# First loads by k tile, two heads side by side in the SSD product, and a boundary and a last tile moved: a two-layer hybrid trunk on one core

## The chip, the core and the metric

The kernel runs on one core of a Trainium2 chip. The metric is the device time of one execution in microseconds (us), as the median of several runs. Engines are called PE (TensorE; PEld is its weight load), DVE (VectorE), ACT (ScalarE), POOL (GpSimd) and SP (SyncE, which here only issues DMAs).

## What is computed

Two layers of a hybrid decoder, batch 1, 256 tokens, width 1024, all in float32. With 256 tokens there is one attention block and one SSD chunk, so the block selection and the state carried between chunks fall away:

```python
h = rms_norm(x, ln_w); proj = h @ w_in          # q, k, v, gate, z, x/B/C, dt
q, k = rms_norm(q, q_norm_w), rms_norm(k, k_norm_w)
attn = softmax(causal(q @ k.T - slope * distance)) @ v * silu(g_attn)   # 8 heads of 128
xs, bm, cm = split(silu(causal_conv4(xbc)))
dt = softplus(dt_raw + dt_bias); a_cs = cumsum(-exp(a_log) * dt)
decay = exp(where(causal, a_cs[l] - a_cs[s], -inf))
y = (cm @ bm.T * decay) @ (xs * dt) + d_skip * xs                       # 16 heads of 64
y = rms_norm(y * silu(z), groups=2)
x = x + concat(attn, y) @ w_out
```

## The kernel before, in words

Every large product is made of three fp32r matmuls, because each operand is split into a rounded part and the rest: high by high, low by high, high by low. Class `Weights` loads the weights in pieces of two k tiles (`raw`, 348 or 512 columns) into four buffers by DMAs on SP's queue (L78), casts a piece on ACT to `wh` (L92) and subtracts on DVE to `wl` (L94); pieces 0 and 4 are subtracted on POOL (`ON_POOL`). A `raw` buffer comes free when its subtraction is done, and then the next load is issued. Up to eight pieces are kept ready.

At the start SP issues the transposed x (`xT`, four DMAs of two k tiles) and `raw` 0 to 3 in turns, then x itself (`x_sb`); ACT issues one DMA for all parameters (`par_sb`, L136). Ten warm-up matmuls run meanwhile (L152). `first_tokens` (L277) makes `hr` (ACT, scaled by `ln_w`) and `lr` (DVE: `xT` is multiplied in place, then `hr` is subtracted), two k tiles at a time. The v columns are computed from these at once, in three groups v0, v1, v2, without the rms scale; `first_scale` (L287) takes the scale `rs0` from x on ACT, DVE and POOL, and the v results leave PSUM with it (L572). `first_norm` (L297) spreads the scale by a matmul with ones (`rg`, L307) and makes `hT` and `lT`, which all other products of the layer read.

In the SSD part four heads make a quarter (`ssd_quarter`): for each head a product of 256 columns (`e_lo`, L481) and one of 128 columns (`e_hi`, L483), both with 64 weight columns, go to one half of the partitions of `yp`. Each is fp32 and runs as two passes in the trace.

At the end of a layer W_out is read in three stages `oa`, `ob`, `oc`; token half t = 0 is finished first. `pre_norm` (L241) then norms the new x: `hn` on DVE and ACT, `yield wait`, eight transposes on PE (`tp`, L263), `hw` on DVE, `hT` on ACT, `lT` on DVE. A wait counts calls of `tick`, one for each piece of weights. Outside the regions of `manual_schedule` the framework's scheduler sets the order on each engine, and `urgent()` raises a priority in it. Each DMA signals one of eight semaphores (`DMAHW0` to `DMAHW7`), and the ninth waits until the first that used the same one has landed.

Of the kernel before, what the change touches and what calls it, by code (L numbers as in the profile page):

```python
# [15 lines left out]
P = 128  # L16
S = 256
# [31 lines left out]
class Weights:  # L49
# [22 lines left out]
    def load(self, upto):  # L72
        while self.nload <= min(upto, len(self.loads) - 1):
            off, wd = self.loads[self.nload]
            n = KR * wd
            t = self.raw_pool.tile([P, KR, 512], F32, tag="raw", name=f"raw{self.nload}")
            src = self.w[off:off + P * n].rearrange("(p k n) -> p k n", p=P, k=KR)
            self.nc.sync.dma_start(t[:, :, :wd], src)  # L78
            self.raw[self.nload] = t
            self.nload += 1  # L80

    def pump(self, upto=None):
        nc = self.nc
        upto = len(self.subs) if upto is None else upto
        while self.prepped < upto and self.prepped - self.freed < NB:
            i = self.prepped
            li, s, wd = self.subs[i]
            self.load(li + (RAWB - 1 if s == 0 else RAWB - 1))
            src = self.raw[li][:, s * KS:(s + 1) * KS, :wd]
# [18 lines left out]
WARM = 10  # L108
ON_POOL = (0, 4)
URGENT = 400  # L110
# [3 lines left out]
def hybrid_kernel(ctx: ExitStack, tc: tile.TileContext, x, par, w, out):  # L114
# [24 lines left out]
    for s in range(KT // KS):  # L139
# [58 lines left out]

    def mm_tokens(L, name, ts, lh, ll, pss, start, stop, last):

        i0 = ws.index[(L, name)]
        k0, kt, wd = next((k, n, c) for nm, k, n, c in CHUNKS if nm == name)
        for s in range(kt // KS):
            ws.pump()
            wh, wl = ws.parts[i0 + s]
            for t, ps in zip(ts, pss):
                tl = slice(t * P, (t + 1) * P)
                for kk in range(KS):
                    kl = k0 % KT + s * KS + kk
                    first = start and s == 0 and kk == 0  # L210
                    final = stop and s * KS + kk == kt - 1
                    pe.matmul(ps[:, :wd], lh[:, kl, tl], wh[:, kk, :wd], start=first, stop=False)  # L212
                    pe.matmul(ps[:, :wd], ll[:, kl, tl], wh[:, kk, :wd], start=False, stop=False)  # L213
                    pe.matmul(ps[:, :wd], lh[:, kl, tl], wl[:, kk, :wd], start=False, stop=final)  # L214
            if last:
# [61 lines left out]
    def first_tokens(s, hr, lr):  # L277

        ks = slice(s * KS, (s + 1) * KS)
# [17 lines left out]
    def first_norm(rs, hT, lT):  # L297
# [149 lines left out]
    def ssd_quarter(L, pr, x2, dth, ac, nac, cb, cm, dsh):  # L447
# [27 lines left out]
        for i in range(2):  # L475
            for r in range(2):
                j = 2 * i + r
                h = 4 * pr + j
                xs = slice(j * 64, (j + 1) * 64)
                o = slice(r * 64, (r + 1) * 64)  # L480
# [51 lines left out]
    for L in range(NL):  # L532
        pc = L * NPAR
        if L == 0:
# [3 lines left out]
            lv = keep.tile([P, KT, S], F32R, tag="kT", name="lr")  # L538
            with tc.manual_schedule(engines={mybir.EngineType.Activation, mybir.EngineType.DVE}):
                for s in range(KT // KS):  # L540
                    first_tokens(s, hv, lv)
                    ws.pump(s + 1)
            rs0 = small.tile([P, 2], F32, tag="rs0", name="rs0", bufs=1)
# [101 lines left out]

        po = {}
        for j in range(2):
            for t in range(2):
                po[t, j] = ps_p.tile([P, 512], F32, tag="ps_p", name=f"o{t}{j}")
                mm_tokens(L, f"oa{j}", (t,), ah, al, (po[t, j],), True, False, t == 1)  # L650
        drain()
        for j in range(2):
            for t in range(2):
                mm_tokens(L, f"ob{j}", (t,), sh, sl, (po[t, j],), False, False, t == 1)
        region = tc.manual_schedule(engines={mybir.EngineType.PE})
        for t in range(2):
# [3 lines left out]
            for j in range(2):  # L660
                mm_tokens(L, f"oc{j}", (t,), sh, sl, (po[t, j],), False, True, t == 1)
                for a, b in [(0, 256), (256, 512)] if L == NL - 1 and t == j == 1 else [(0, 512)]:
                    cs = slice(j * 512 + a, j * 512 + b)
                    xs = x_sb[t][:, cs]
                    with urgent():
                        dve.tensor_tensor(xs, xs, po[t, j][:, a:b], ALU.add)
                    if L == NL - 1:
# [66 lines left out]
```

## Time and profile before

| what | us |
|---|---|
| three runs, median | 463.7 |
| lowest and highest run | 462.63, 464.36 |
| the profiled execution's own time | 463.97 |
| its span, first to last instruction | 461.9 |
| PE busy in the span | 451.5 |
| DVE busy | 348.0 |
| ACT busy | 280.3 |
| POOL busy | 31.6 |

The profile is of one execution. Times in it count from the first instruction; some 2 us lie around the span. Matmuls are pipelined: one of 512 columns is shown longer than the distance to the next, so costs are read from starts. In a timeline row the brackets give the engine's idle time before the row and what ended it.

### The profile page before, as it was taken

Reading aid. Unit: us, or ns where it says so; the run is one execution under the profiler, and the core shown is the slowest. Engines: PE = TensorE matmul, PEld = TensorE weight load, DVE = VectorE, ACT = ScalarE, POOL = GpSimd, SP = SyncE. Lnnn points to the kernel's source line nnn. Section 1 sums busy time; section 2 is a strip of 40 time slices with the busy share of each in tenths; the row PEclk is TensorE's granted clock in tenths of the full one; section 3 lists DMA queues with packets and bytes.
Section 4 is the critical chain, followed back from the end, with each engine's and each line's share of the span. In section 5 each row is a group of like instructions: output and inputs, shape, how many; then the busy total and the mean of one; then the engine's idle time right before and its main releaser. Section 6 shows DMA issues by size and latency. Waiting matters only on the chain.

```text
span 461.9 us, 7752 instructions
## 1 busy us (share of the span) xinstructions
PE 451.5 (98%) x2900; PEld 403.7 (87%) x2900; DVE 348.0 (75%) x625; ACT 280.3 (61%) x567; POOL 31.6 (7%) x31
## 2 busy tenths in 40 slices
PE   5999999999999999999999999999999999999996
PEld 5998878899998999888799977889999888998885
DVE  4877854889999878957366685776999898789611
ACT  5757758896668546535355765977767674555400
POOL 2200210200000000110000021020000000011000
PEclk8899999999999999999999999999999999999999
DMA  8688884632453355555164988561525263455201
GB/s 268 201 260 286 282 315 181 228 95 95 168 158 115 103 184 181 183 182 142 48 181 128 311 266 305 203 206 62 162 85 188 92 184 115 143 199 176 99 23 70
DMA packets 26213, 79.43 MB, mean 172 GB/s; under 512 B 2592, under 2 KB 9152, under 8 KB 25664
## 3 DMA queue, kind: packets, MB, share of 16 engines
q1 hardware_dynamic: 26032, 78.82, 52.2%
q8 instruction: 23, 0.38, 0.3%
q14 instruction: 14, 0.11, 0.1%
q10 hardware_dynamic: 144, 0.12, 0.1%
HBM read 77.85 MB, written 1.08 MB: 171 GB/s over the span
## 4 chain that ended last, share of the span: by engine, by line
PE 91%; DMA 3%; DVE 3%; ACT 1%; POOL 1%; issue 0%; SPq 0%; DVEq 0%; POOLq 0%
PE o L212 6%; PE o L214 6%; PE o L213 6%; PE xb L231 4%; PE xb L232 4%; PE xb L230 4%; PE z L231 3%; PE z L232 3%; PE k L212 3%; PE g L230 3%; PE g L232 3%; PE q L213 3%; PE k L213 3%; PE g L231 3%; PE z L230 3%; PE k L214 3%
## 5 line engine op out<-in xcount | busy, mean ns | idle before, releaser
L92 ACT CAST wh<-raw 128x1024 fp32r<-128x1024 f32 (+2 forms) x144 | 144.3, 1004 | 68.6 <-PE o L213 21.5
L94 DVE TENSOR_TENSOR wl<-raw,wh 128x1024 fp32r<-128x1024 f32 (+2 forms) x142 | 164.2, 1167 | 28.3 <-ACT wh L92 27.1
L230 PE MATMUL xb<-hT,wh 128*128 128x256 f32 x192 | 56.0, 292 | 0.0
L231 PE MATMUL xb<-lT,wh 128*128 128x256 f32 x192 | 54.9, 286 | 0.0
L232 PE MATMUL xb<-hT,wl 128*128 128x256 f32 x192 | 54.6, 285 | 0.0
L230 PEld LDWEIGHTS xb<-hT,wh 128*128 128x128 f32 x192 | 36.3, 189 | 0.3
L231 PEld LDWEIGHTS xb<-lT,wh 128*128 128x128 f32 x192 | 36.2, 189 | 0.2
L232 PEld LDWEIGHTS xb<-hT,wl 128*128 128x128 f32 x192 | 36.2, 189 | 0.1
L231 PE MATMUL g<-lT,wh 128*128 128x256 f32 x128 | 36.0, 281 | 0.0
L230 PE MATMUL g<-hT,wh 128*128 128x256 f32 x128 | 35.9, 280 | 0.0
L232 PE MATMUL g<-hT,wl 128*128 128x256 f32 x128 | 35.8, 280 | 0.0
L231 PE MATMUL z<-lT,wh 128*128 128x256 f32 x128 | 35.7, 279 | 0.0
L232 PE MATMUL z<-hT,wl 128*128 128x256 f32 x128 | 35.6, 278 | 0.0
L230 PE MATMUL z<-hT,wh 128*128 128x256 f32 x128 | 35.5, 277 | 0.0
L431 DVE SCALAR_TENSOR_TENSOR cv<-rw,par_sb,cv 128x256 f32<-128x256 f32 x72 | 31.5, 479 | 4.8 <-ACT cv L428 4.8
L172 POOL TENSOR_TENSOR rr<-se,mhalf 128x4 f32<-128x4 f32 x16 | 18.0, 1123 | 126.5 <-DVE se L328 90.7
L212 PE MATMUL k<-wh,hT 128*128 128x512 f32 x64 | 25.5, 398 | 0.0
L212 PE MATMUL o<-wh,ah 128*128 128x512 f32 x64 | 25.5, 398 | 0.0
L213 PE MATMUL k<-wh,lT 128*128 128x512 f32 x64 | 25.4, 397 | 0.0
L214 PE MATMUL k<-wl,hT 128*128 128x512 f32 x64 | 25.3, 395 | 0.0
L213 PE MATMUL o<-wh,al 128*128 128x512 f32 x64 | 25.2, 394 | 0.0
L212 PE MATMUL o<-wh,sh 128*128 128x512 f32 x64 | 25.2, 394 | 0.0
(182 smaller groups left out, 1123.3 us busy)
## 6 DMA issues: line engine op xcount, KB each, us to landing
raw<-in_w_dram SPq DMA_DIRECT2D x120, 512.0 KB, 4.4
raw<-in_w_dram SPq DMA_DIRECT2D x16, 348.0 KB, 3.7
cb<-cd SPq DMA_DIRECT2D x4, 1024.0 KB, 8.3
raw<-in_w_dram SPq DMA_DIRECT2D x8, 344.0 KB, 4.0
xT<-in_w_dram SPq DMA_DIRECT2D x4, 256.0 KB, 5.6
x<-in_x_dram SPq DMA_DIRECT2D x2, 512.0 KB, 7.5
out_dram<-x SPq DMA_DIRECT2D x3, 256.0 KB, 2.0
out_dram<-x SPq DMA_DIRECT2D x2, 128.0 KB, 1.8
```

What stands on the lines that cost most here:

```text
L92: nc.scalar.copy(h[:, :, :wd], src)
L94: sub.tensor_tensor(lo[:, :, :wd], src, h[:, :, :wd].bitcast(F32), ALU.subtract)
L172: pool.tensor_tensor(o, i, mhalf[:, :n], ALU.pow)
L212: pe.matmul(ps[:, :wd], lh[:, kl, tl], wh[:, kk, :wd], start=first, stop=False)
L213: pe.matmul(ps[:, :wd], ll[:, kl, tl], wh[:, kk, :wd], start=False, stop=False)
L214: pe.matmul(ps[:, :wd], lh[:, kl, tl], wl[:, kk, :wd], start=False, stop=final)
L230: pe.matmul(o, wh[:, kk, cs], lh[:, k, :], start=(k == 0 and c == 0), stop=False)
L231: pe.matmul(o, wh[:, kk, cs], ll[:, k, :], start=False, stop=False)
L232: pe.matmul(o, wl[:, kk, cs], lh[:, k, :], start=False, stop=(k == KT - 1 and c == 1))
L431: dve.scalar_tensor_tensor(cv[:, c, :], rw[:, c, k:k + S], cw(k), cv[:, c, :], ALU.mult, ALU.add)
```

## The change

- **First loads.** `raw` 0 comes by k tile (two DMAs on SP); `xT` moves to ACT's queue, in five DMAs, with a small DMA of `ln_w` of layer 0 between. x and the rest of the parameters are issued on SP behind `raw` 6.
- **First work.** Piece 0 is cast and subtracted by k tile; all subtractions are on DVE. `lr` is made in one DVE operation for a k tile, so `xT` stays unscaled and `first_norm` multiplies by `ln_w` and the scale in eight operations of one k tile instead of two of four.
- **Table.** A one-column Tanh on ACT (`table`) stands ahead of the first real activation.
- **SSD product.** The two heads of a pair take turns: both long products, then both short ones.
- **Boundary.** The waits of `pre_norm` go from 2 to 3 (t = 0) and from 7 to 5 (t = 1).
- **Last columns.** The last output tile of the last layer is computed as two of 256 columns in two PSUM banks, one after the other in each stage.

```diff
+            for ks in self.steps(self.nload):
+                self.nc.sync.dma_start(t[:, ks, :wd], src[:, ks, :])
+    def steps(i):
+        return [slice(k, k + 1) for k in range(KR)] if i == 0 else [slice(0, KR)]
...
-            nc.scalar.copy(h[:, :, :wd], src)
-            sub = nc.gpsimd if i in ON_POOL else nc.vector
-            sub.tensor_tensor(lo[:, :, :wd], src, h[:, :, :wd].bitcast(F32), ALU.subtract)
+            for ks in self.steps(i):
+                nc.scalar.copy(h[:, ks, :wd], src[:, ks, :wd])
+                nc.vector.tensor_tensor(lo[:, ks, :wd], src[:, ks, :wd],
+                                        h[:, ks, :wd].bitcast(F32), ALU.subtract)
...
-    nc.scalar.dma_start(par_sb, par)
+    nc.scalar.dma_start(xT[:, 0:1, :], xsrc[:, 0:1, :])
+    nc.scalar.dma_start(par_sb[:, C_LN:C_LN + KT], par[:, C_LN:C_LN + KT])
+    nc.scalar.dma_start(xT[:, 1:2, :], xsrc[:, 1:2, :])
+    for s in range(1, KT // KS):
         ks = slice(s * KS, (s + 1) * KS)
-        nc.sync.dma_start(xT[:, ks, :], xsrc[:, ks, :])
-        ws.load(s)
-    for t in range(2):
-        nc.sync.dma_start(x_sb[t], x[t * P:(t + 1) * P, :])
+        nc.scalar.dma_start(xT[:, ks, :], xsrc[:, ks, :])
+    ws.load(RAWB - 1)
...
+    table = const.tile([P, 1], F32, name="table")
+    act.activation(table, ones[:, 0:1], AF.Tanh)
...
         for k in range(s * KS, (s + 1) * KS):
-            act.activation(hr[:, k, :], xT[:, k, :], AF.Copy, scale=par_sb[:, C_LN + k:C_LN + k + 1])
-        dve.tensor_tensor(xT[:, ks, :], xT[:, ks, :],
-                          par_sb[:, C_LN + s * KS:C_LN + (s + 1) * KS].unsqueeze(2)
-                          .to_broadcast([P, KS, S]), ALU.mult)
-        dve.tensor_tensor(lr[:, ks, :], xT[:, ks, :], hr[:, ks, :].bitcast(F32), ALU.subtract)
+            ln = par_sb[:, C_LN + k:C_LN + k + 1]
+            act.activation(hr[:, k, :], xT[:, k, :], AF.Copy, scale=ln)
+            dve.scalar_tensor_tensor(lr[:, k, :], xT[:, k, :], ln, hr[:, k, :].bitcast(F32),
+                                     ALU.mult, ALU.subtract)
...
-            dve.tensor_tensor(xT[:, ks, :], xT[:, ks, :],
-                              rg[:, 0:S].unsqueeze(1).to_broadcast([P, 4, S]), ALU.mult)
+            for k in range(half * 4, half * 4 + 4):
+                dve.scalar_tensor_tensor(xT[:, k, :], xT[:, k, :], par_sb[:, C_LN + k:C_LN + k + 1],
+                                         rg[:, 0:S], ALU.mult, ALU.mult)
...
         for i in range(2):
-            for r in range(2):
-                j = 2 * i + r
-                pe.matmul(yp[o, i * S:(i + 1) * S], xd[:, 0, xs], e_lo[:, j, :],
-                          start=True, stop=False)
-                pe.matmul(yp[o, i * S + 128:(i + 1) * S], xd[:, 1, xs], e_hi[:, j, :],
-                          start=False, stop=True)
+            for hi in range(2):
+                for r in range(2):
+                    j = 2 * i + r
+                    c0 = i * S + hi * P
+                    pe.matmul(yp[o, c0:(i + 1) * S], xd[:, hi, xs],
+                              e_hi[:, j, :] if hi else e_lo[:, j, :],
+                              start=(hi == 0), stop=(hi == 1))
...
-            resume(pre_norm(L, 1, hT, lT, msum[1], 7))
+            resume(pre_norm(L, 1, hT, lT, msum[1], 5))
...
+                po[t, j] = [((0, 512), ps_p.tile([P, 512], F32, tag="ps_p", name=f"o{t}{j}"))]
+                if L == NL - 1 and t == j == 1:
+                    po[t, j] = [((0, 256), po[t, j][0][1]), ((256, 512), bank("o11b"))]
...
-                resume(pre_norm(L + 1, 0, hT, lT, msum[0], 2))
+                resume(pre_norm(L + 1, 0, hT, lT, msum[0], 3))
```

**Order on ACT at the start**, with the semaphores that an instruction waits for (`DMAHW` of a DMA's landing). Before:

```order
L136 DMA par_sb<-in_par_dram 128x236
L281 ACT_TABLE_LOAD [waits DMAHW1_49]
L281 ACTIVATE hr<-xT,par_sb 128x256 [waits DMAHW0_49]
L394 ACTIVATE ea<-par_sb 128x16
L92 CAST wh_139<-raw_90 128x2x348 [waits DMAHW2_49]
```

With the change:

```order
L144 DMA xT<-in_w_dram 128x256
L145 DMA par_sb<-in_par_dram 128x8
L146 DMA xT<-in_w_dram 128x256
L149 DMA xT<-in_w_dram 128x512
L149 DMA xT<-in_w_dram 128x512 [waits DMAHW1_49]
L149 DMA xT<-in_w_dram 128x512 [waits DMAHW2_49]
L156 ACT_TABLE_LOAD
L156 ACTIVATE table<-ones 128x1 [waits DVE_49]
L290 ACTIVATE hr<-xT,par_sb 128x256 [waits DMAHW3_49,DMAHW0_49]
L290 ACTIVATE hr<-xT,par_sb 128x256 [waits DMAHW5_49]
L99 CAST wh_141<-raw_94 128x348 x2
```

The table load stood behind one DMA issue and the wait for the first `xT`; now it stands behind six issues, the last two of which wait for `DMAHW1` and `DMAHW2`. Those are the two halves of `raw` 0, as DVE's subtractions of them show:

```order
L100 TENSOR_TENSOR wl_142<-raw_94,wh_141 128x348 [waits DMAHW1_49,Activation_49]
L100 TENSOR_TENSOR wl_142<-raw_94,wh_141 128x348 [waits DMAHW2_49,Activation_49]
```

**Order on PE in a quarter of the SSD product** (`cb` is `e_lo`, `ehi` is `e_hi`; layer 0, third quarter). Before:

```order
L230 MATMUL g_1943<-hT_129,wh_1604 128x256
L481 MATMUL yp<-cb_0_193,xd 64x256
L466 MATMUL xtp<-ident,x_0_946 128x128
L483 MATMUL yp<-ehi_0_1572,xd 64x128
L481 MATMUL yp<-cb_0_193,xd 64x256
```

With the change:

```order
L240 MATMUL g_1957<-lT_132,wh_1660 128x256
L490 MATMUL yp<-cb_0_201,xd 64x256 x2
L490 MATMUL yp<-ehi_0_1586,xd 64x128 x2
L490 MATMUL yp<-cb_0_201,xd 64x256 x2
L490 MATMUL yp<-ehi_0_1586,xd 64x128 x2
L474 MATMUL xtp<-ident,x_0_960 128x128 x4
```

Before, in all eight quarters, a transpose or a full-width matmul stands behind the first long product. With the change five quarters stand in one piece as here; the other three (layer 0 first, layer 1 first and second) still have two transposes behind the first long product.

**Order on PE at the boundary**, from the transposes of t = 1 to the first v matmuls of t = 1. Before:

```order
L212 MATMUL v_2716<-wh_2655,hT_2568 128x348
L263 MATMUL tp<-ident,hn 128x128 x8
L213 MATMUL v_2716<-wh_2655,lT_2569 128x348
L214 MATMUL v_2716<-wl_2656,hT_2568 128x348
L212 MATMUL v_2716<-wh_2687,hT_2568 128x348
L213 MATMUL v_2716<-wh_2687,lT_2569 128x348
...
L212 MATMUL v_2760<-wh_2501,hT_2568 128x348
L212 MATMUL v_2804<-wh_2631,hT_2568 128x348
L213 MATMUL v_2760<-wh_2501,lT_2569 128x348
```

With the change:

```order
L221 MATMUL v_2730<-wh_2701,hT_2582 128x348
L272 MATMUL tp<-ident,hn 128x128 x8
L222 MATMUL v_2730<-wh_2701,lT_2583 128x348
L223 MATMUL v_2730<-wl_2702,hT_2582 128x348
L221 MATMUL v_2774<-wh_2515,hT_2582 128x348
L221 MATMUL v_2818<-wh_2645,hT_2582 128x348
L222 MATMUL v_2774<-wh_2515,lT_2583 128x348
```

Eight matmuls of t = 0 stood between the transposes and the first matmul that reads their result; now two do. On ACT both copies of v's t = 0 results now stand ahead of the `hT` casts, where one did before. The transposes of t = 0 move from behind the second piece of `oc0` to behind its third.

## Rows read from the trace of the kernel before

**Rows 1.** The page, part 1: busy time of each engine.

```profile
PE 451.5 (98%) x2900; PEld 403.7 (87%) x2900; DVE 348.0 (75%) x625; ACT 280.3 (61%) x567; POOL 31.6 (7%) x31
```

**Rows 2.** Waits of PE: us in total, times, longest.

```profile
PE v L212 <- ACT wh L92: 3.5, 2, 3.2
...
PE tp L263 <- DVE hn L253: 0.8, 1, 0.8
...
PE v L214 <- DVE wl L94: 0.2, 1, 0.2
```

**Rows 3.** Windows: busy (count) of PE, PEld, DVE, ACT, POOL; granted clock; DMA.

```profile
12.00:14.00 2.00, 2.00 (x9) 2.00 (x8) 1.97 (x4) 1.49 (x4) 0.00 (x0) 0.50 1.00 354
14.00:16.00 2.00, 2.00 (x14) 2.00 (x14) 1.97 (x4) 1.98 (x7) 0.00 (x0) 0.96 0.68 193
```

**Rows 4.** Timeline of ACT at the start: start, us.

```profile
5.12 1.28 ACT L281 ACT_TABLE_LOAD   x1 [5.12 <-DMA xT<-in_w_dram]
...
7.33 0.76 ACT L92 CAST wh<-raw 128x696 fp32r<-128x696 f32 x1
```

**Rows 5.** Timeline of PE at the start.

```profile
8.14 0.95 PE L212 MATMUL v<-wh,hr 128*128 128x348 f32 x2 [3.23 <-ACT wh L92]
...
10.35 0.66 PE L214 MATMUL v<-wl,hr 128*128 128x348 f32 x1 [0.58 <-POOL wl L94]
```

**Rows 6.** Chain that ended last, to 27 us: start, us, what.

```profile
0.73 4.51 DMA par_sb<-in_par_dram
...
5.26 0.55 SPq L78
...
5.85 7.16 DMA x<-in_x_dram
...
17.79 0.56 POOL rs L172
```

**Rows 7.** DMA issues, the one at 1.18 us: KB, us to landing.

```profile
raw<-in_w_dram SPq DMA_DIRECT2D x1, 348.0 KB, 5.4
```

**Rows 8.** Timeline of PE, first quarter of the SSD product, layer 0.

```profile
136.88 0.65 PE L481 MATMUL yp<-cb,xd 128*64 128x256 f32 x2
137.45 0.44 PE L364 MATMUL pp<-ident,sc 128*128 128x128 f32 x2
137.82 0.32 PE L483 MATMUL yp<-ehi,xd 128*64 128x128 f32 x1
137.83 0.43 PE L481 MATMUL yp<-cb,xd 128*64 128x256 f32 x1
137.98 0.27 PE L483 MATMUL yp<-ehi,xd 128*64 128x128 f32 x1
...
139.27 0.39 PE L232 MATMUL g<-hT,wl 128*128 128x256 f32 x1
```

**Rows 9.** Timeline of PE at the boundary of the layers.

```profile
242.62 1.03 PE L263 MATMUL tp<-ident,hn 128*128 128x128 f32 x8
243.41 0.41 PE L213 MATMUL v<-wh,lT 128*128 128x348 f32 x1
...
244.77 0.48 PE L212 MATMUL v<-wh,hT 128*128 128x348 f32 x2
245.38 0.42 PE L213 MATMUL v<-wh,lT 128*128 128x348 f32 x1
```

**Rows 10.** Timeline of ACT at the boundary.

```profile
243.98 1.22 ACT L272 CAST hT<-hw 128x512 fp32r<-128x512 f32 x2 [3.11 <-DVE hw L266]
245.10 0.44 ACT L574 COPY v<-v 128x348 f32<-128x348 f32 x1
```

**Rows 11.** Timeline of SP, the last two output DMAs.

```profile
458.58 0.81 SPq L668 DMA_DIRECT2D out_dram<-x  x2
```

**Rows 12.** Chain that ended last, whole span: shares of 461.9 us by line.

```profile
by line: PE o L212 6.2%; PE o L214 6.2%; PE o L213 6.1%; PE xb L231 4.5%; PE xb L232 4.4%; PE xb L230 4.4%; PE z L231 3.3%; PE z L232 3.2%; PE k L212 3.2%; PE g L230 3.2%; PE g L232 3.2%; PE q L213 3.2%; PE k L213 3.2%; PE g L231 3.2%; PE z
```

**Rows 13.** The page, part 5: a DVE group of fused operations on 256 columns.

```profile
L431 DVE SCALAR_TENSOR_TENSOR cv<-rw,par_sb,cv 128x256 f32<-128x256 f32 x72 | 31.5, 479 | 4.8 <-ACT cv L428 4.8
```

More of the change, by code (lines that the diff above doesn't have):

```diff
@@ L77, in load @@
             src = self.w[off:off + P * n].rearrange("(p k n) -> p k n", p=P, k=KR)
-            self.nc.sync.dma_start(t[:, :, :wd], src)
+            for ks in self.steps(self.nload):
+                self.nc.sync.dma_start(t[:, ks, :wd], src[:, ks, :])
             self.raw[self.nload] = t
             self.nload += 1
+    @staticmethod
+    def steps(i):
+        return [slice(k, k + 1) for k in range(KR)] if i == 0 else [slice(0, KR)]
     def pump(self, upto=None):
@@ L87, in pump @@
             li, s, wd = self.subs[i]
-            self.load(li + (RAWB - 1 if s == 0 else RAWB - 1))
-            src = self.raw[li][:, s * KS:(s + 1) * KS, :wd]
+            self.load(li + RAWB - 1)
+            src = self.raw[li]
             h = self.wh_pool.tile([P, KS, 512], F32R, tag="wh", name=f"wh{i}")
             lo = self.wl_pool.tile([P, KS, 512], F32R, tag="wl", name=f"wl{i}")
-            nc.scalar.copy(h[:, :, :wd], src)
-            sub = nc.gpsimd if i in ON_POOL else nc.vector
-            sub.tensor_tensor(lo[:, :, :wd], src, h[:, :, :wd].bitcast(F32), ALU.subtract)
+            for ks in self.steps(i):
+                nc.scalar.copy(h[:, ks, :wd], src[:, ks, :wd])
+                nc.vector.tensor_tensor(lo[:, ks, :wd], src[:, ks, :wd],
+                                        h[:, ks, :wd].bitcast(F32), ALU.subtract)
             self.parts[i] = (h, lo)
@@ L108 @@
 WARM = 10
-ON_POOL = (0, 4)
 URGENT = 400
@@ L197, in drain, with mm_tokens @@
             tick()
-    def mm_tokens(L, name, ts, lh, ll, pss, start, stop, last):
+    def mm_tokens(L, name, ts, lh, ll, pss, start, stop, last, cols=None):
         i0 = ws.index[(L, name)]
         k0, kt, wd = next((k, n, c) for nm, k, n, c in CHUNKS if nm == name)
+        cs = slice(*cols) if cols else slice(0, wd)
         for s in range(kt // KS):
@@ L211, in mm_tokens @@
                     final = stop and s * KS + kk == kt - 1
-                    pe.matmul(ps[:, :wd], lh[:, kl, tl], wh[:, kk, :wd], start=first, stop=False)
-                    pe.matmul(ps[:, :wd], ll[:, kl, tl], wh[:, kk, :wd], start=False, stop=False)
-                    pe.matmul(ps[:, :wd], lh[:, kl, tl], wl[:, kk, :wd], start=False, stop=final)
+                    pe.matmul(ps[:, cs], lh[:, kl, tl], wh[:, kk, cs], start=first, stop=False)
+                    pe.matmul(ps[:, cs], ll[:, kl, tl], wh[:, kk, cs], start=False, stop=False)
+                    pe.matmul(ps[:, cs], lh[:, kl, tl], wl[:, kk, cs], start=False, stop=final)
             if last:
@@ L475, in ssd_quarter @@
         for i in range(2):
[L476 to L484 removed]
+            for hi in range(2):
+                for r in range(2):
+                    j = 2 * i + r
+                    xs = slice(j * 64, (j + 1) * 64)
+                    o = slice(r * 64, (r + 1) * 64)
+                    c0 = i * S + hi * P
+                    pe.matmul(yp[o, c0:(i + 1) * S], xd[:, hi, xs],
+                              e_hi[:, j, :] if hi else e_lo[:, j, :],
+                              start=(hi == 0), stop=(hi == 1))
         for i in range(2):
@@ L538, in hybrid_kernel @@
             lv = keep.tile([P, KT, S], F32R, tag="kT", name="lr")
-            with tc.manual_schedule(engines={mybir.EngineType.Activation, mybir.EngineType.DVE}):
+            with tc.manual_schedule(engines={mybir.EngineType.Activation, mybir.EngineType.DVE,
+                                             mybir.EngineType.SP}):
                 for s in range(KT // KS):
@@ L542, in hybrid_kernel @@
                     ws.pump(s + 1)
+                for t in range(2):
+                    nc.sync.dma_start(x_sb[t], x[t * P:(t + 1) * P, :])
+                nc.sync.dma_start(par_sb[:, 0:C_LN], par[:, 0:C_LN])
+                nc.sync.dma_start(par_sb[:, C_LN + KT:], par[:, C_LN + KT:])
             rs0 = small.tile([P, 2], F32, tag="rs0", name="rs0", bufs=1)
@@ L646, in hybrid_kernel, with mm_out @@
         po = {}
+        def mm_out(name, t, j, lh, ll, start, stop):
+            for i, (c, ps) in enumerate(po[t, j]):
+                mm_tokens(L, name, (t,), lh, ll, (ps,), start, stop,
+                          t == 1 and i == len(po[t, j]) - 1, c)
         for j in range(2):
             for t in range(2):
-                po[t, j] = ps_p.tile([P, 512], F32, tag="ps_p", name=f"o{t}{j}")
-                mm_tokens(L, f"oa{j}", (t,), ah, al, (po[t, j],), True, False, t == 1)
+                po[t, j] = [((0, 512), ps_p.tile([P, 512], F32, tag="ps_p", name=f"o{t}{j}"))]
+                if L == NL - 1 and t == j == 1:
+                    po[t, j] = [((0, 256), po[t, j][0][1]), ((256, 512), bank("o11b"))]
+                mm_out(f"oa{j}", t, j, ah, al, True, False)
         drain()
@@ L653, in hybrid_kernel @@
             for t in range(2):
-                mm_tokens(L, f"ob{j}", (t,), sh, sl, (po[t, j],), False, False, t == 1)
+                mm_out(f"ob{j}", t, j, sh, sl, False, False)
         region = tc.manual_schedule(engines={mybir.EngineType.PE})
@@ L660, in hybrid_kernel @@
             for j in range(2):
-                mm_tokens(L, f"oc{j}", (t,), sh, sl, (po[t, j],), False, True, t == 1)
-                for a, b in [(0, 256), (256, 512)] if L == NL - 1 and t == j == 1 else [(0, 512)]:
+                for i, ((a, b), ps) in enumerate(po[t, j]):
+                    mm_tokens(L, f"oc{j}", (t,), sh, sl, (ps,), False, True,
+                              t == 1 and b == 512, (a, b))
                     cs = slice(j * 512 + a, j * 512 + b)
@@ L665, in hybrid_kernel @@
                     with urgent():
-                        dve.tensor_tensor(xs, xs, po[t, j][:, a:b], ALU.add)
+                        dve.tensor_tensor(xs, xs, ps[:, a:b], ALU.add)
                     if L == NL - 1:
```

2 lines of the change are left out of this document (removed).

## The prediction

> **What bounds the kernel now.** I read the busy times first: PE works in 451.5 of 461.9 us [rows 1], so a change pays where it shortens PE's own work or one of its few waits. Then the waits of PE [rows 2]: 3.5 us in two waits for the cast of a weight piece (the first, of 3.2, ends with the very first product; the other, 0.3, comes later), 0.2 for a subtraction on DVE, and 0.8 for `hn` at the boundary of the layers; the timeline adds 0.58 for POOL's subtraction of the first piece [rows 5]. Then the granted clock: it is 0.50, the level of 1.2 GHz, until shortly after 14 us, and 2.4 GHz behind that [rows 3]. So the program has four places to gain: the start up to some 25 us, the SSD quarters (PE is busy there, but with half its columns), the boundary, and the tail behind the last matmul. Supply is no limit elsewhere; DVE, the next engine, is busy for 75% [rows 1].
>
> **The start.** Before, ACT waits until 5.12 for `xT`, loads its table in 1.28, needs 0.93 from there to the cast (`hr` of two tiles and one small activation), and casts in 0.76 [rows 4]; PE begins at 8.14 [rows 5]. The dummy is there to take the 1.28 out of this row. The order on ACT says that it won't: ahead of the table load stand six DMA issues, and the fifth and sixth wait until the first and second half of `raw` 0 have landed. That an issue really stands still for a landing is seen in the chain: the ninth DMA went out at 5.26, when `par_sb`, issued at 0.73, had taken its 4.51 [rows 6].
>
> When does the second half of `raw` 0 land? The first 256 KB on SP were in at 5.1, when ACT's wait for them ended [rows 4], beside 118 KB on ACT; the next 348 KB, issued at 1.18, landed 5.4 later, at 6.6 [rows 7]. So 374 KB were in by 5.1 and 722 KB by 6.6. Now 348 KB on SP go beside 132 KB on ACT: 480 KB, in between at 5.55. The two rows bound it, 5.1 and 6.6. From there: the last issue 0.55 [rows 6], table 1.28, the dummy about 0.1 (an estimate, since it is one column), 0.93 for `hr`, half a cast about 0.45, and 0.05 from cast to matmul as before. That is 3.36, so PE begins at **8.9** (8.5 to 10.0), later than 8.14.
>
> What PE loses by that it gains at once. The 0.58 on POOL goes: the subtraction is DVE's now and by halves, and DVE makes `lr` with one operation of 0.48 a tile [rows 13] where it read `xT` twice. So PE's work up to 14 us is that of a start at 8.14 + 0.58 = 8.72 before and 8.9 now, at half clock: 0.1 worse. The later waits of 0.2 and 0.3 [rows 2] hang on the two POOL subtractions (the second freed its buffer late, which delayed piece 8) and go too. **Start: -0.4.** With the bounds of the landing it is -0.6 to +0.1.
>
> Moved behind `raw` 6, x lands later. At 0.93 + 0.76 a piece [rows 4] ACT ends the third cast at about 12.6, DVE then frees the buffer near 13.6, and the second half of x is issued near 14.7. This I cost at nothing: `rs0` is first needed when PE meets the `rg` matmuls, 84 products after its start, at about 24.4 (18 at 0.29 up to 14.2, which is 348 columns at 1.2 GHz, then 66 at 0.15 to 0.16). The cover is looked at again below. `first_norm` now takes eight operations of 0.48, 3.8 us [rows 13], where two stood; nothing reads `hT` until the 144 v products are through, at about 35, and without that cover the two us more would show.
>
> **The SSD quarters.** In the first quarter a first long product runs alone from 136.88 to 137.45, two transposes follow, and from 137.82 the halves run side by side: the short product of head 0 begins at 137.82 and the long one of head 1, in the other half of the columns, at 137.83 [rows 8]. From there to 139.27 it takes 1.44 for long, short, long, short of one column half (0.43 + 0.21 twice, and the change back). Where both long products stand together the whole quarter costs that: the 0.57 of the lone long product goes, and of the 0.37 for the two transposes all but their own 0.2 (0.10 each, from the eight in 0.79 of [rows 9]). That saves 0.73 in each of the five quarters that now stand in one piece. In the three where two transposes still follow the first long product, the path through head 1 is as long as before: nothing. **5 x 0.73 = -3.7.** Below it is bounded by no overlap of two long products, above by the same 0.73 in all eight, -5.8.
>
> Head 1's first pass starts at 137.83, ahead of head 0's second pass at 137.98 [rows 8], though it stands behind it in the program: the two halves of the columns are not held to one order. The Trainium skill, "TensorE: Matmul & The Clock Gate", Part 3, says that packed matmuls start and end strictly in program order; here the trace differs, and what the rule would give is the first rival below.
>
> **The boundary.** The transposes of t = 0 come one piece, six matmuls of 0.22, later. `hn` was 0.8 late [rows 2], 1.3 of work now cover it: **-0.8**. For t = 1 the order shows the opposite of the smaller number 5: two matmuls now stand behind the transposes, not eight. Before, with X the start of the transposes at 242.62, PE went on at X + 0.79, the first `hT` casts began at X + 1.36, and the first product with `lT` at X + 2.76 [rows 9, 10]. Now the copy of v in front of the casts waits for the last of the two products, until about X + 1.3, and takes 0.44 [rows 10]: the casts begin at X + 1.7, and the product with `lT` at X + 3.1. Up to there PE had the transposes and ten products of 0.16 or 0.17 (eight in 1.36), 2.4 of 2.76; now the transposes and four, 1.4 of 3.1. The idle time goes from 0.4 to 1.7: **+1.3**. Together **+0.5**. If the chip gets `hT` sooner than this, the bound is -0.8.
>
> **The tail.** The last two output issues took 0.81 behind each other [rows 11]; now the first of them is long out when the last matmul ends: **-0.4**. The halved tile needs 96 products of 256 columns for 48 of 512. A 256-column line costs 4.5% of 461.9 for 192, 0.108 each; a 512-column line 6.2% for 128, 0.224 [rows 12]. Halves are no dearer.
>
> **Sum.** -0.4 - 3.7 + 0.5 - 0.4 = -4.0 against the profiled execution's own 463.97: 460.0. That execution lies 0.3 over the median 463.7, so the median becomes **459.7**. A measurement of this kernel can tell about 0.5%, 2.3 us: 461.4 is the line for faster.
>
> **The rivals.**
>
> - *Strict order on PE.* If PE starts passes in the order of the program, whichever half of the columns they use, a long product of head 1 cannot begin before the second pass of head 0's. In each quarter that puts a long pass (0.21) and a short one (0.11) on the path, 0.32 of the 0.73. The saving is 2.1 instead of 3.7: **461.3**. Against it stand the starts of [rows 8]. Chance 0.08.
> - *The clock rises earlier.* Before, PE ran without a gap from 10.35 on [rows 5], and the clock was up shortly after 14 [rows 3]. Now it would run without one from 8.9. If the clock rises those 1.5 earlier, half of them is won, and an early landing gives 0.2 more: **458.7**. For it: no gap is left; against it: the first product is no earlier. Chance 0.2.
> - *Layer 0 gets new waits.* There the order is new on PE, ACT and DVE, not only at the places named. Two us of waits in the attention part, like the 0.8 at the boundary a few times over, give **461.6**. Layer 1 keeps its order. Chance 0.11.
> - *Slower: x comes too late.* By the nearest row x takes 7.16 to land [rows 6]: issued at 14.7, at 21.9. Before, 5.3 passed from its first landing to the second `rs` (13.01 to 18.35) [rows 6]. At worst then `rs0` is there at 27.2, and PE stands 2.8 at the `rg` matmuls from 24.4. A pause of 3.23 at the start [rows 5] came with a half clock until 14 us, about 6 us that cost 3; with that the kernel takes 465.5. From a pause of 3.3 on it is at 466, slower by more than 0.5%. Against it: much of the 5.3 was DVE and POOL at other work, and x is issued when only `raw` 7 and small DMAs follow. Chance 0.05.
> - *Nothing overlaps.* If two long products slow each other to half speed, the 3.7 go and 463.3 is left. Chance 0.03; [rows 8] shows a long and a short one together without that.
>
> **How the numbers follow.** My forecast has 0.53; its own range is 458.4 (no idle time at t = 1) to 460.8 (late landing, and a product side by side slower than reckoned). Faster: the forecast, the clock, and half of the strict order, 0.76. Same: the rest of it, layer 0 and nothing overlaps, with the milder end of a late x, 0.20. Slower: 0.04. The range goes from 457.2 (early clock and no idle time at t = 1) to 461.9 (new waits in layer 0).
>
> **What would show it.** Right: the table load on ACT starts near 6, not before 4; PE begins at 8.9; five quarters take about 1.5 from the first long product to the next full-width matmul and three keep 2.4; PE idles over 1 us behind the transposes of t = 1 and not in front of those of t = 0. Wrong: a table load that ends before `xT` lands, a first product before 8, quarters of 1.8 or more, or a wait of PE at `rg`.

## The result, and the profile after

| what | before | with the change |
|---|---|---|
| median of the runs beside it, us | 463.47 | 459.33 |
| its runs | 462.63 to 464.36 | 459.04 to 460.53 |
| the profiled execution's own time | 463.97 | 459.08 |
| its span | 461.9 | 457.3 |

The ratio is 0.9915 (95% interval 0.9889 to 0.9942). The forecast was 459.7, the range 457.2 to 461.9. The same kernel was run again later, beside the last experiments: 460.05, ratio 0.992 (0.9892 to 0.9949). All ten of its runs lie between 458.8 and 461.4, with a median of 459.8. So the time came out as forecast; not all of its parts did, as the profile shows.

The page's first part answers to [rows 1]. PE is still the bound; the 3.4 us that it is busy less is less than the 4.6 that the span lost.

```profile
PE 448.1 (98%) x2948; PEld 406.1 (89%) x2948; DVE 346.9 (76%) x634; ACT 279.9 (61%) x569; POOL 25.8 (6%) x29
```

The waits of PE (us in total, times, longest), against [rows 2]. The waits for `wl` are gone, and so is the one for `hn`. The one for `sc` (the first softmax row of layer 0) has grown from 0.3, and one for `hT` (the boundary) is new.

```profile
PE v L221 <- ACT wh L99: 2.7, 1, 2.7
PE pp L372 <- DVE sc L367: 1.1, 1, 1.1
PE v L221 <- ACT hT L281: 1.1, 1, 1.1
PE warm L160 <- DVE ones L154: 1.1, 1, 1.1
```

**The start**, timeline (start, us; in brackets the idle time before and what ended it), against [rows 4, 5]. The table load starts when `raw` 0 has landed, as the order on ACT said, but at 5.32 and not near 6; the first product comes at 8.04.

```profile
5.32 1.28 ACT L156 ACT_TABLE_LOAD   x1 [5.32 <-DMA raw<-in_w_dram]
...
6.72 0.90 ACT L290 ACTIVATE hr<-xT,par_sb 128x256 fp32r<-128x256 f32 x2
...
7.52 0.85 ACT L99 CAST wh<-raw 128x348 fp32r<-128x348 f32 x2
8.04 0.54 PE L221 MATMUL v<-wh,hr 128*128 128x348 f32 x1 [2.72 <-ACT wh L99]
```

The windows (busy and count of PE, PEld, DVE, ACT, POOL; granted clock; DMA) show the clock back at 2.4 GHz before 12 us, where [rows 3] had it at 1.2 GHz until 14. In the timeline the products stand 0.29 apart until 11.56 and 0.16 from 11.76 on. PE has no gap behind its first product.

```profile
8.00:10.00 2.00, 1.96 (x7) 1.96 (x8) 1.90 (x6) 1.86 (x4) 0.00 (x0) 0.55 0.90 324
10.00:12.00 2.00, 2.00 (x10) 2.00 (x9) 1.82 (x4) 1.78 (x4) 0.00 (x0) 0.60 0.79 219
12.00:14.00 2.00, 2.00 (x15) 2.00 (x14) 2.00 (x4) 1.94 (x4) 0.00 (x0) 1.00 0.67 184
```

**A quarter of the SSD product** in one piece, timeline of PE, layer 0, against [rows 8]: from the `g` product at 148.12 to the transposes at 149.78 it is 1.66, less the 0.11 of that product 1.55. Long and short products now come in fours, two passes of each head.

```profile
148.12 0.28 PE L240 MATMUL g<-lT,wh 128*128 128x256 f32 x1
148.33 0.65 PE L490 MATMUL yp<-cb,xd 128*64 128x256 f32 x4
148.81 0.39 PE L490 MATMUL yp<-ehi,xd 128*64 128x128 f32 x4
149.03 0.60 PE L490 MATMUL yp<-cb,xd 128*64 128x256 f32 x4
149.47 0.39 PE L490 MATMUL yp<-ehi,xd 128*64 128x128 f32 x4
149.78 0.44 PE L474 MATMUL xtp<-ident,x 128*128 128x128 f32 x2
```

Five quarters take 1.55 and three 2.26, where before six took 2.27 and two 2.33: 3.75 less in all.

**Behind the last quarter** of a layer something else has changed. The two fences are the timelines of PE in layer 1, before and after: the second product of `z` behind the quarter, and the one 20 products later. Before it is 391.30 to 393.57, 0.1135 a product; after 386.14 to 388.49, 0.1175.

```profile
391.30 0.28 PE L230 MATMUL z<-hT,wh 128*128 128x256 f32 x1
...
393.57 0.28 PE L232 MATMUL z<-hT,wl 128*128 128x256 f32 x1
```

```profile
386.14 0.28 PE L241 MATMUL z<-hT,wl 128*128 128x256 f32 x1
...
388.49 0.28 PE L240 MATMUL z<-lT,wh 128*128 128x256 f32 x1
```

PE doesn't wait there and the granted clock is 1.00 in both. The slower pace costs some 4.5 ns a product over long stretches. It holds for 136 products in layer 0 and 163 in layer 1 without a break: 1.35 us.

**The boundary**, timeline of PE against [rows 9]: no idle time in front of the transposes of t = 0 (226.34); behind those of t = 1 PE waits 1.06 and later 0.14.

```profile
226.34 1.03 PE L272 MATMUL tp<-ident,hn 128*128 128x128 f32 x8
...
238.71 1.03 PE L272 MATMUL tp<-ident,hn 128*128 128x128 f32 x8
...
241.12 0.59 PE L221 MATMUL v<-wh,hT 128*128 128x348 f32 x2 [1.06 <-ACT hT L281]
```

**The first softmax row.** The decay factors go to DRAM and back (4.3 and 6.8 us in the chain of waits, from 60.05), and ACT stands still until they are there (`cb`). In the timeline of ACT that is at 71.37 before (first fence) and at 71.27 after (second), although PE had the layer's v products behind it some 3 us sooner. PE's wait for the row grows from 0.29 to 1.06 (third and fourth fence: PE before, PE after).

```profile
71.37 2.46 ACT L454 ACTIVATE ehi<-cb,nac 128x128 f32<-128x128 f32 x8 [4.75 <-DMA cb<-cd]
```

```profile
71.27 2.46 ACT L462 ACTIVATE ehi<-cb,nac 128x128 f32<-128x128 f32 x8 [4.13 <-DMA cb<-cd]
```

```profile
91.26 0.30 PE L364 MATMUL pp<-ident,sc 128*128 128x128 f32 x1 [0.29 <-DVE sc L359]
```

```profile
90.20 0.30 PE L372 MATMUL pp<-ident,sc 128*128 128x128 f32 x1 [1.06 <-DVE sc L367]
```

### The profile page after: what moved, and what is told of

Read it like the earlier page. It is cut to its first block, busy times and chain, and to the rows that moved or that the text cites. A ratio compares the mean times of both kernels' runs of the same rounds, so it can differ in the third digit from the quotient of the medians.

```text
span 457.3 us, 7867 instructions
## 1 busy us (share of the span) xinstructions
PE 448.1 (98%) x2948; PEld 406.1 (89%) x2948; DVE 346.9 (76%) x634; ACT 279.9 (61%) x569; POOL 25.8 (6%) x29
## 4 chain that ended last, share of the span: by engine, by line
PE 79%; DMA 9%; ACT 6%; DVE 4%; issue 1%; POOL 0%; SPq 0%; ACTq 0%; POOLq 0%
PE o L221 6%; PE o L223 6%; PE o L222 6%; PE xb L240 4%; PE xb L241 4%; PE xb L239 4%; DMA raw<-in_w_dram 4%; PE z L240 3%; PE z L239 3%; PE g L239 3%; PE z L241 3%; PE g L240 3%; PE g L241 3%; PE yp L490 3%; ACT wh L99 2%; DVE wl L100 2%
## 5 line engine op out<-in xcount | busy, mean ns | idle before, releaser
L100 DVE TENSOR_TENSOR wl<-raw,wh 128x1024 fp32r<-128x1024 f32 (+3 forms) x145 | 166.0, 1156 | 33.4 <-ACT wh L99 31.3
L99 ACT CAST wh<-raw 128x1024 fp32r<-128x1024 f32 (+3 forms) x145 | 143.8, 999 | 61.4 <-DMA raw<-in_w_dram 15.5
L221 PE MATMUL q<-wh,hT 128*128 128x512 f32 x64 | 25.3, 396 | 0.0
L222 PE MATMUL q<-wh,lT 128*128 128x512 f32 x64 | 25.2, 394 | 0.0
L223 PE MATMUL q<-wl,hT 128*128 128x512 f32 x64 | 24.9, 394 | 0.0
L221 PE MATMUL o<-wh,ah 128*128 128x512 f32 (+1 forms) x64 | 24.5, 384 | 0.0
```

The source lines that it names most:

```text
L99: nc.scalar.copy(h[:, ks, :wd], src[:, ks, :wd])
L100: nc.vector.tensor_tensor(lo[:, ks, :wd], src[:, ks, :wd], h[:, ks, :wd].bitcast(F32), ALU.subtract)
L221: pe.matmul(ps[:, cs], lh[:, kl, tl], wh[:, kk, cs], start=first, stop=False)
L222: pe.matmul(ps[:, cs], ll[:, kl, tl], wh[:, kk, cs], start=False, stop=False)
L223: pe.matmul(ps[:, cs], lh[:, kl, tl], wl[:, kk, cs], start=False, stop=final)
```

## The experiments

Three questions were left: whether the quarters pay what they save, what the start is worth, and where its gain goes. The runs of one group share a chip and the runs of the kernel before (463.72, 463.48 and 463.93 us in the three groups).

### Heads in turns alone (e1_turns_alone)

The kernel before, with only the loop of the SSD product changed. On PE hardly anything else moves; four quarters stand in one piece.

```diff
-            for r in range(2):
-                j = 2 * i + r
...
+            for hi in range(2):
+                for r in range(2):
+                    j = 2 * i + r
```

> The kernel before with the heads in turns and nothing else. Four quarters then stand in one piece, four are still chopped. The forecast's step: 4 x 0.73 = 2.9 less, 460.6 us. The rival, from the trace of the change: the z products behind the last quarter of each layer go at 0.118 each instead of 0.113, some 160 products, 0.7 a layer, so the last quarters win nothing in the end: 2.9 - 1.4 = 1.5 less, 462.0 us, with quarters of 1.55 all the same. Strict order on PE: 4 x 0.41 = 1.6 less with quarters of 1.86.

Measured: 461.61 us, ratio 0.9963 (0.9948 to 0.9978), so 1.0 to 2.4 less. Four quarters take 1.55 and four 2.26, 3.0 less in all. The forecast's step would have given 2.9; the interval excludes it. The `z` products of layer 1 show why (timeline of PE, again 20 products apart: 388.51 to 390.86, 0.1175 each):

```profile
388.51 0.28 PE L232 MATMUL z<-hT,wl 128*128 128x256 f32 x1
...
390.86 0.28 PE L231 MATMUL z<-lT,wh 128*128 128x256 f32 x1
```

The slower pace comes with the turns alone. Strict order on PE would have made quarters of 1.86, and falls.

### The last quarter in the old order, and reversed (e8, e7)

The change, with the last quarter of each layer as before (e8), or with its heads in the order 1, 0 (e7):

```diff
-            for hi in range(2):
-                for r in range(2):
+            for hi, r in (((0, 0), (1, 0), (0, 1), (1, 1)) if pr == 3 else
+                          ((0, 0), (0, 1), (1, 0), (1, 1))):
```

```diff
-                for r in range(2):
+                for r in ((1, 0) if pr == 3 else (0, 1)):
```

> The change with the last quarter of each layer in the old order of heads, which a z product cuts again. The forecast's step (each whole quarter saves 0.73): 1.45 more, 460.8 us. Theory: the quarter takes 2.33 again but the z products go back to 0.113, 136 and 163 of them, 1.35 less: no change, 459.3 to 459.5 us.

> The change with the two heads of each pair in the other order in the last quarter of each layer; the quarter stays whole. If the pace of the z products behind it (0.118 instead of 0.113) hangs on which half of the columns ends last, it goes back to 0.113 and the kernel gains 1.4: 457.9 us. If it hangs on the quarter being whole, nothing: 459.3 us.

Measured: 460.06 (0.9894 to 0.9949) and 460.52 (0.9901 to 0.9948), against the change's 459.3 and 460.05: no difference that can be told from none. In the trace the two part. With the old order the quarter takes 2.33 and the `z` products 0.113 (timeline of PE, 20 apart: 388.17 to 390.43); reversed, the quarter takes 1.55 and they take 0.118 as in the change.

```profile
387.95 0.38 PE L241 MATMUL z<-hT,wl 128*128 128x256 f32 x1
388.17 0.28 PE L239 MATMUL z<-hT,wh 128*128 128x256 f32 x1
...
390.43 0.28 PE L241 MATMUL z<-hT,wl 128*128 128x256 f32 x1
```

So the pace of `z` does not hang on the order of the heads, and it costs nearly what the whole quarter saves (0.78 against some 0.6 in layer 0 and 0.7 in layer 1): two of the five quarters win next to nothing.

Whether the quarter is whole does not decide it either. In layer 0 of e10 and e11 (below) a `z` product cuts the last quarter, but behind two long products and not behind one, and `z` goes at 0.118 all the same (timeline of PE in e10; the last two rows are 20 products apart):

```profile
162.59 0.65 PE L490 MATMUL yp<-cb,xd 128*64 128x256 f32 x4
163.17 0.38 PE L240 MATMUL z<-lT,wh 128*128 128x256 f32 x1
...
164.72 0.28 PE L239 MATMUL z<-hT,wh 128*128 128x256 f32 x1
...
167.08 0.28 PE L241 MATMUL z<-hT,wl 128*128 128x256 f32 x1
```

One thing fits all 28 last quarters of the 14 profiles: where the two heads end side by side, as in the change, `z` goes at 0.118; where one head ends alone, as at the end of [rows 8], it goes at 0.113. That is a regularity and not a cause; why PE then goes at the other pace is open.

### The start alone (e2_start_alone)

The change, with the SSD loop, the boundary's waits and the last tile of the kernel before. The diff shows the waits; the loop and the tile go back as they stood.

```diff
...
-            resume(pre_norm(L, 1, hT, lT, msum[1], 5))
+            resume(pre_norm(L, 1, hT, lT, msum[1], 7))
...
-                resume(pre_norm(L + 1, 0, hT, lT, msum[0], 3))
+                resume(pre_norm(L + 1, 0, hT, lT, msum[0], 2))
```

> The change with the heads, the boundary and the last columns as before: the first loads, the first work and the dummy alone. The forecast's step: 0.4 less, 463.1 us. Theory from the trace of the change: 0.1 from the first product, 0.6 from the wait for POOL, 0.5 from the later waits, 1.0 from the clock that rises at 11.6 instead of 14.2, and 0.8 given back in a wait of PE for a softmax row near 90: 1.4 to 1.7 less, about 461.9 us. The table load still starts when the second half of raw 0 has landed (5.3).

Measured: 463.13, ratio 0.9979 (0.9963 to 0.9995). The median agrees with the forecast's step, but it stands between two groups: five of the twelve runs lie at 461.4 to 462.2 and seven at 463.1 to 464.2. The profiled one, at 461.57, is of the lower group and fits the other theory. Its windows show the clock back before 12 us:

```profile
8.00:10.00 2.00, 1.74 (x6) 1.74 (x7) 1.22 (x3) 1.08 (x4) 0.00 (x0) 0.50 0.94 350
10.00:12.00 2.00, 2.00 (x11) 2.00 (x10) 1.77 (x3) 1.54 (x5) 0.00 (x0) 0.69 0.80 223
```

What the upper group does was not seen. The traces show one thing that differs between executions of nearly the same start: the products go from 0.29 apart to 0.16 at 11.0 here, at 11.6 in the change, and at 13.3 and 13.6 in e4 and e8, with first products at 7.9 to 8.3 in all. So the start is worth between nothing and 2 us. That this moment parts the two groups is not shown: half clock up to 13.6 instead of 11.0 costs 1.3, and the groups are some 2 apart.

### More warm-up products (e3_warm16)

```diff
-WARM = 10
+WARM = 16
```

> The change with 16 warm-up products instead of 10, so that PE works until about 7.9 instead of 5.3. If the half clock from 8.0 to 11.6 comes from the pause of 2.7 in front of the first product, it stays at full: 3.5 us at half clock cost 1.75, so 1.2 to 1.75 less, 457.6 to 458.1 us (less, if the casts are then late). If the clock is half for another reason, or the supply of pieces is the bound up to 12, no change: 459.3 us.

Measured: 459.15 (0.9882 to 0.9912): no change against the change's own runs. The clock does stay at 2.4 GHz from the first product, at 7.58. But PE then waits for the second piece, and longer at the softmax row (waits of PE; the 1.1 for `hT` and `ones` are as in the change):

```profile
PE pp L372 <- DVE sc L367: 1.5, 1, 1.5
...
PE v L221 <- ACT wh L99: 0.7, 1, 0.7
PE v L223 <- DVE wl L100: 0.2, 1, 0.2
PE sp L354 <- ACT kT L347: 0.2, 1, 0.2
```

### The table load ahead of the waiting issues (e5_table_first)

```diff
-    for s in range(1, KT // KS):
-        ks = slice(s * KS, (s + 1) * KS)
-        nc.scalar.dma_start(xT[:, ks, :], xsrc[:, ks, :])
-    ws.load(RAWB - 1)
...
-    act.activation(table, ones[:, 0:1], AF.Tanh)
+    with tc.manual_schedule(engines={mybir.EngineType.Activation}):
+        nc.scalar.dma_start(xT[:, 2:4, :], xsrc[:, 2:4, :])
+        act.activation(table, ones[:, 0:1], AF.Tanh)
+        for s in range(2, KT // KS):
+            ks = slice(s * KS, (s + 1) * KS)
+            nc.scalar.dma_start(xT[:, ks, :], xsrc[:, ks, :])
+    ws.load(RAWB - 1)
```

> The change with the dummy and its table load ahead of the last two xT issues on ACT, so that they no longer stand behind the landing of raw 0. The table then loads from about 2.6 to 3.9 and the first product comes when its x is there, near 5.7, right behind the warm-ups. If the blocked dummy costs what the forecast's step says (8.9 instead of some 6), the kernel gains 1.5 us or more: 457.8. If the next pieces bind (the xT of the second piece lands at 8.3, its cast ended at 9.9), PE only waits later, as with 16 warm-ups: 459.0 to 459.5 us.

Measured: 460.74 (0.9901 to 0.9957), six runs from 458.16 (the profiled one) to 461.85. The table loads at 2.62 and the first product comes at 6.71, 1.3 earlier than in the change; then PE waits for the second piece, whose `xT` lands near 8 as in the change (timeline):

```profile
2.62 1.28 ACT L152 ACT_TABLE_LOAD   x1 [2.62 <-issue]
...
6.71 0.43 PE L223 MATMUL v<-wh,hr 128*128 128x348 f32 x1 [1.68 <-ACT wh L99]
...
7.95 0.91 ACT L292 ACTIVATE hr<-xT,par_sb 128x256 fp32r<-128x256 f32 x2 [0.91 <-DMA xT<-in_w_dram]
...
9.58 0.43 PE L223 MATMUL v<-wh,hr 128*128 128x348 f32 x1 [0.69 <-ACT wh L99]
```

The blocked dummy, which the forecast made so much of, costs the kernel nothing that can be measured: the next pieces bind.

### The wait of t = 0 back at 2 (e4_wait2)

```diff
-                resume(pre_norm(L + 1, 0, hT, lT, msum[0], 3))
+                resume(pre_norm(L + 1, 0, hT, lT, msum[0], 2))
```

> The change with the wait of t = 0 back at 2; t = 1 stays at 5. In the written order the transposes of t = 1 then have eight products behind them again, as in the kernel before. If the wait of t = 0 sets both places: the idle time in front of the transposes of t = 0 comes back (0.8), the idle time behind those of t = 1 falls from 1.2 to 0.1 to 0.4: 0.0 to 0.4 less, 458.9 to 459.3 us. The forecast's terms (0.8 against 1.3) give 0.5 less. If the waits are hidden by what follows, no change at either place.

Measured: 459.82 (0.9899 to 0.9928), no difference. In the trace the two places change over as expected (timeline of PE): 0.77 in front of t = 0, nothing above 0.13 behind t = 1.

```profile
227.53 1.09 PE L272 MATMUL tp<-ident,hn 128*128 128x128 f32 x8 [0.77 <-DVE hn L262]
...
240.37 1.03 PE L272 MATMUL tp<-ident,hn 128*128 128x128 f32 x8
```

So it was the 3 for t = 0 that took the cover from t = 1. Beside a 2 for t = 0, a 5 (here) and a 7 (the kernel before, e2) for t = 1 leave the same waits of 0.77 and 0.13; a 7 beside the 3 was not run.

### The last tile whole (e6_last_whole)

The change, with the last output tile as one of 512 columns, as in the kernel before.

> The change with the last output tile in one piece of 512 columns, as before. The forecast's step: 0.4 more, 459.7 us. Theory from the trace: the last issue comes 0.7 later behind the last matmul, but the 96 halves (0.119 each) against 48 whole ones (0.229) cost 0.4, so 0.3 more, 459.6 us; by the rival, in which the halves cost what the tail wins, no change.

Measured: 460.23 (0.9899 to 0.9943): inconclusive. In the traces the last product starts 33.41 behind the last `np` product (of the norm of y) with the whole tile and 33.82 with halves (in the change and in its second profile), 0.41 more; from there to the end of the span it is 4.04 with the whole tile and 3.45 with halves, 0.59 less. By the traces the last columns are worth 0.2.

### A shorter way to the decay factors, and two steps more (e9 to e12)

The change once more (e9); the softplus on DVE with five terms of its series instead of nine (e10); that, and PE kept in the program's order in the first two groups of v products of t = 0 of layer 1 (e11); all of it with the table load of e5 and 14 warm-ups (e12).

```diff
-        dve.tensor_scalar(pl, z2, 1.0 / 17.0, None, ALU.mult)
-        for i in range(7, 0, -1):
+        dve.tensor_scalar(pl, z2, 1.0 / 9.0, None, ALU.mult)
+        for i in range(3, 0, -1):
```

```diff
-                mm_tokens(L, f"v{c}", ts, hv, lv, pss, True, True, ts[-1] == 1)
+                if L == 1 and c < 2 and ts == (0,):
+                    with tc.manual_schedule(engines={mybir.EngineType.PE}):
+                        mm_tokens(L, f"v{c}", ts, hv, lv, pss, True, True, False)
+                else:
+                    mm_tokens(L, f"v{c}", ts, hv, lv, pss, True, True, ts[-1] == 1)
```

> The change itself once more, as the neighbour of the next three. By its four runs so far, 459.3 us; by the three kernels close to it (last tile whole, last quarter reversed or old), which lay at 460.1 to 460.5, 460.0 us. The half clock should end anywhere between 11 and 13.6, and PE's waits near 78 and 91 should be the longer the earlier the work in front of them is done: together 1.0 to 2.7 us.

> The change with four terms fewer in the series for softplus (5 of 9; the terms left out are under 1e-6). In the written order the cumulative sum (cp) then comes 17 rows of PE earlier, about 3.9 us, and with it the trip of the decay through DRAM for which ACT stands still at 67 to 71. If that trip is what PE's waits near 78 and 91 hang on, they fall from 1.1 to 2.7 us to under 0.5: 1.0 us or more less than the change beside it. If they hang on DVE and the pieces of weights, no change.

> The same, and PE keeps the program's order in the v products of t = 0 of layer 1, so that the transposes of t = 1 stand 18 products (2.8 us) ahead of the first product that needs them. The idle time of 1.20 behind them should go: 1.2 us less than the kernel with the short series. If the casts are then late for another reason, less than half of that.

> The same, with the table load ahead of the last two xT issues and 14 warm-up products. The first product comes at 6.7 at full clock, so up to 12 us PE is 1.2 to 1.8 ahead; with the trip through DRAM out of the way this should now reach the end in part: 0.5 to 1.5 us less than the kernel without. If the trip or the pieces still bind, no change.

| run | us | ratio to before, 95% | `cb` back (ACT) | PE's waits for `kT` and `sc` | idle behind t = 1 |
|---|---|---|---|---|---|
| e9 | 460.05 | 0.9892 to 0.9949 | 72.17 | 0.62, 1.33 | 1.06, 0.14 |
| e10 | 461.21 | 0.9919 to 0.9961 | 67.22 | 0, 0.78 | 1.06, 0.13 |
| e11 | 460.02 | 0.9893 to 0.9949 | 67.50 | 0, 1.20 | none |
| e12 | 459.45 | 0.9878 to 0.9939 | 70.80 | 0, 0.41 | none |

In e9, the same kernel as the change, the factors come back and the first softmax row is there at these times (timelines of ACT and PE):

```profile
72.17 0.99 ACT L462 ACTIVATE ehi<-cb,nac 128x128 f32<-128x128 f32 x3 [5.36 <-DMA cb<-cd]
...
91.10 0.30 PE L372 MATMUL pp<-ident,sc 128*128 128x128 f32 x1 [1.33 <-DVE sc L367]
```

The row comes 18.93 behind the factors, as in the change (71.27 to 90.20). It is 18.92 or 18.93 in all eight profiles with this order (the change, e2 and e4 to e9), though the factors come back anywhere from 70.35 (e5) to 73.69 (e7): there PE's wait for `sc` hangs on the trip through DRAM.

With the factors back 5 us sooner in e10 than in e9 the wait for `kT` goes, and the one for `sc` falls by 0.55. The row comes only 2.4 sooner: the chain in front of it now runs over PE's `k` products, ACT and DVE, and no longer over the trip. In e11, with the factors back at 67.50, the wait for `sc` is 1.20 again. The kernel is not faster for it. The order of layer 0 shifted with the series: the second quarter is chopped again (2.26) and the fourth is cut by a `z` product (1.90), 1.1 more by the starts, and in the profile the half clock lasted until 13.6. So the expected 1.0 didn't come, and e10 doesn't test its size. The early transposes of e11 do what was expected: the idle time is gone, and the median falls by 1.2, though the two intervals still overlap. In e12 the start is again early (7.19) and PE again waits for the second piece (1.35); its v products end at 35.52, against 34.14 in e10, with one q product more done by then. Its 459.45 is the lowest of its group, but its interval overlaps that of the change: no version here is shown to beat it.

## Why the prediction was right, and where it was not

| step | forecast | measured |
|---|---|---|
| the start, to the last v product of layer 0 | -0.4 | -3.0 (profile); -2.3 and -2.1 in e4 and e8, where the clock rose at 13.3 and 13.6 (0.23 of each is a q product done earlier) |
| waits of PE in layer 0 | 0 | +0.8 (+1.7 in the second profile) |
| SSD quarters | -3.7 | -3.75 |
| pace of `z` behind the last quarters | 0 | +1.35 |
| boundary | +0.5 | +0.3 |
| tail and last tile | -0.4 | -0.3 |

The rows (of the change's own profile) sum to -4.6, the difference of the spans. The sum leaves out that the q and k products of layer 0 also go at 0.233 instead of 0.229 in this profile, +0.45 for 109 of them, and that other short stretches change pace the other way.

**The quarters** came as worked out, place by place: five at 1.55, three as before. The rival of strict order would have given 1.86. By that rule, in the Trainium skill, "TensorE: Matmul & The Clock Gate", Part 3, packed products start strictly in program order. The trace of the change disagrees if each pass counts by itself: the first pass of head 1 starts at 148.34 and the second pass of head 0 at 148.60. Whole products start in order there. In the quarter of [rows 8], before, not even these do: a long product of the third head starts at 138.09, and the short one of the second head, ahead of it in the program, at 138.31 (timeline of PE):

```profile
138.09 0.59 PE L481 MATMUL yp<-cb,xd 128*64 128x256 f32 x3
138.31 0.48 PE L483 MATMUL yp<-ehi,xd 128*64 128x128 f32 x3
```

But the step took it that what follows a quarter costs the same as before, and it doesn't (e1, e8): of the 3.7 some 2.4 is left.

**The start** is the step that failed in size. Its mechanism held: the dummy's table load stands behind the landing of `raw` 0. Its landing was mis-sized: reckoned by bytes at 5.55, which with the last issue makes 6.1. The two halves took 3.2 us each from their issue (page, DMA issues) and the last issue was through at 5.32.

```profile
raw<-in_w_dram SPq DMA_DIRECT2D x2, 174.0 KB, 3.2
```

So the first product came at 8.04 and not at 8.9. And the clock rose earlier, a rival with a chance of 0.2: in the profile 13 products take 3.7 us (8.04 to 11.76), where 17 took 6.1 before, 0.58 of it idle; at 0.16 each that is 1.6 lost against 2.8. The rival's reason is not borne out: e4 and e8 have no gap behind their first product either, and there the clock rose at 13.3 and 13.6. With 0.1 for the first product, 0.58 for POOL and 0.5 for the later waits this makes 2.4 of the 3.0; the rest was not taken apart.

**The rival of new waits in layer 0** came true as well, in one place rather than several: the start's gain runs up against the decay factors, which come back at 71.3, as before. That wait (+0.8), the pace of `z` (+1.35) and the start's surplus (-2.6) cancel but for some 0.4. The forecast had them at nothing, so that the total came out so near is in part luck. It was right in its sum and in its quarters, boundary and tail, not in its start. Run alone, the turns (e1, 2.1 less) and the start (e2, 0.6 less) make 2.7 of the change's 4.1; the intervals are too wide to say whether they add up.

**The boundary** came as the order showed: -0.77 and +1.07 against -0.8 and +1.3. **The tail**: halves are dearer after all, 0.41, against the row by which they cost nothing [rows 12]. The halves go at the slower pace, 0.118, and at 0.1133 two would have cost no more than the 0.229 of a whole one; the end behind the last product is 0.74 shorter instead of 0.4. **x** was not late in the change, where PE has no wait at `rg`; in e2, e5 and e12 it waits 0.2 to 0.4 there. The rival that ended slower didn't occur.

## What to carry to other kernels

Ask of every gain what is due next: three us won at the start met a chain that starts elsewhere (the softplus on DVE, and a trip through DRAM), and PE gave back 0.8 to 1.7 of them waiting for that. A reordering of matmuls can change the pace of those behind it; compare starts over a hundred products in both traces before booking what the reordered piece itself saves. And where several parts are changed at once, a total that comes out as forecast proves little: read each term.

## What was not expected of the hardware

- **Two paces of PE at one clock.** Products of 256 columns go 0.1133 or 0.1178 apart, those of 348 columns 0.159 or 0.160 on average, those of 512 0.229 or 0.233, each pace in unbroken stretches of up to 163 products, with no wait and the granted clock at 1.00. The program alone does not set it: the change and e9 are one kernel, with the same order of all 2948 records on PE, and the 105 steps between q and k products in layer 0 take 24.50 us in the change (first fence) and 24.03 in e9 (second). What sets it is open.

```profile
33.20 0.40 PE L221 MATMUL q<-wh,hT 128*128 128x512 f32 x1
...
57.70 0.39 PE L222 MATMUL q<-wh,lT 128*128 128x512 f32 x1
```

```profile
33.34 0.39 PE L221 MATMUL q<-wh,hT 128*128 128x512 f32 x1
...
57.37 0.40 PE L222 MATMUL q<-wh,lT 128*128 128x512 f32 x1
```

- **The moment when the clock rises** differs by 2.6 us between executions with first products at 7.9 to 8.3 (11.0 to 13.6). In e6, e7 and e11 the first products, from 8.0 to 8.4 on, stand 0.16 apart, and the half clock comes behind them, from 9.3 to 9.6 until 12.7 to 13.0.
- **A clock row without records.** In e4, e8 and e10 the products stand 0.29 apart, as at half clock, until 13.3 to 13.6, and the windows say 1.00 there. These traces hold no clock record ahead of 13.4 (e4) and 13.6, and a window counts time without a record as full clock. The starts, not the row, tell the pace there.
